# A hybrid attention/RG-LRU step on one core: gate halves evaluated in weight buffers, the first head group's values loaded beside its keys, background sums in 33 places in place of 36

## The chip, the cores and the metric

The kernel runs on one core of a Trainium2 chip. The metric is the device time of one execution in microseconds (us). A core has a matrix engine (TensorE, PE in the profile, with its weight loads as PEld), a vector engine (VectorE, DVE), a scalar engine (ScalarE, ACT), GpSimd (POOL) and SyncE (SP), which here issues most transfers. Each engine works through its own list of instructions in the order of the program and waits on semaphores that the others set.

## The reference

One inference step of two layers in float32. Layer 0 is grouped-query attention over 512 latent and 128 context tokens (16 heads, 4 key/value heads, width 2048), layer 1 a bidirectional gated linear recurrence. The part that the change touches is layer 0's projection, its gate, and the modulation vectors of layer 1, which need only the conditioning vector:

```
m = jax.nn.silu(cond) @ w_mod + b_mod
shift, scale, gate = jnp.split(m[:, None, :], 3, axis=-1)
...
p = h @ w_in
q, k, v, g = jnp.split(p, [ATTN_WIDTH, ATTN_WIDTH + KV_WIDTH, ATTN_WIDTH + 2 * KV_WIDTH], axis=-1)
q = rms_norm(q.reshape(b, n, N_HEADS, HEAD_DIM), q_norm)
k = rms_norm(k.reshape(b, n, N_KV_HEADS, HEAD_DIM), k_norm)
...
keys = jnp.concatenate([ck.astype(k.dtype), k], axis=1)
vals = jnp.concatenate([cv.astype(v.dtype), v], axis=1)
o = blocked_attention(q, keys, vals)
return (o * jax.nn.silu(g)) @ w_out
```

## The kernel before

**Arithmetic.** A float32 product is made of three matmuls: every operand is split into a rounded high part (`hi`, `wh`) and the rest (`lo`, `wl`), and `mm3` adds high x high (L184), and the two mixed products (L185, L186). The activations are split once and stay (`hi`, `lo`). A weight block of 1 MB is loaded by SP into one of four buffers `raw` (`load_w`), and `split_w` makes a high part on ACT (L179) and a low part on DVE (L180) of a half block (128 x 1024) into a ring of three pairs. PE reads these.

**Stages of layer 0's projection.** After the V projection come one K and four Q blocks (`gemm_nat`, four weight blocks each), then eight gate blocks (`gemm_T`, about 430 to 664 us), each of two weight blocks, that is four halves of 48 matmuls of 322 columns. A gate block has two accumulators of 128 gate channels, f = 0 and f = 1; in every half the 24 matmuls of f = 0 come first. Its evacuation `g_evac` computes (tanh(g/2) + 1) g for each f: ACT writes the tanh into a tile `qs` (L491), DVE multiplies into a tile `qf` (L492), and POOL issues the transfer of 322 KB into the scratch `g_s` (L493). `qs` and `qf` are two buffers each in the pool `pb`, shared with the norm and rotary work of K and Q. Then comes the attention: `attn_kv(j)` loads the keys of head group j into a `raw` buffer (`kx`) and its values into a tile of the pool `pc_` (`vx`), `attn_q` loads a head's queries and gate into a `raw` buffer; keys and queries are transposed on PE (L542, L571) and split, scores and softmax (L584 is the exponential) follow.

**Background.** `gemv` computes layer 1's shift and scale on DVE: 32 weight blocks of 1 MB from `w_mod`, in four sections of eight, four sums of 128 x 1024 to a block (L395). At a section's end the two accumulators are split and summed over the partitions by eight matmuls (L403), ACT copies a row (L406), PE transposes it (L408). `background()` is called after each of the 36 weight blocks of K, Q and the gates and takes 32/36 of a step each time; the rest of `gemv` is run after the last.

**What sets the order.** The program is written with pools and tiles; a scheduler lays the instructions of each engine in one list, the splits with higher priority, and inserts the semaphores. A buffer is given again when its last reader is done. So the order in each list depends on which tile waits for which.

Of the kernel before, what the change touches and what calls it, by code (L numbers as in the profile page):

```python
# [9 lines left out]
F32 = mybir.dt.float32  # L10
F32R = mybir.dt.float32r
BF16 = mybir.dt.bfloat16
AF = mybir.ActivationFunctionType
# [8 lines left out]
TW = 644  # L22
TH = TW // 2
# [21 lines left out]
def hybrid_step(ctx: ExitStack, tc: tile.TileContext, i, o):  # L45
    nc = tc.nc
    V, S, G, PE, SY = nc.vector, nc.scalar, nc.gpsimd, nc.tensor, nc.sync
    mult, add, sub = ALU.mult, ALU.add, ALU.subtract

    def pool(name, bufs, space=None, stack=None):  # L50
        kw = {} if space is None else {"space": space}
        return (stack or ctx).enter_context(
            tc.tile_pool(name=name, bufs=bufs, reuse_waits="tile", **kw))
# [3 lines left out]
    rawp = pool("rawp", 4)  # L57
# [6 lines left out]
    g_s = [tc.dram_tile([128, TW], F32, name=f"g_s{h}") for h in range(NH)]  # L64
# [6 lines left out]
    def ps1():  # L71
        return ps.tile([128, 512], F32, name="p1", tag="p1")
# [92 lines left out]
    scale = [cst.tile([128, KT, 2], F32, name=f"scale{l}") for l in range(2)]  # L165
# [68 lines left out]
    def gemm_T(w, col0, after=None):  # L234

        acc = [psd(), psd()]
        for kb in range(2):
            gemm_T_part(acc, load_w(w, kb * 1024, 8, col0, 256), kb * 8)
            if after:
                after()  # L240
        return acc
# [85 lines left out]
    with tc.manual_schedule():  # L327
# [5 lines left out]
        for n in range(9):  # L333
# [26 lines left out]
            if now:  # L360
                for f in range(2):
                    put(n * 2 + f, 0, xt[f], slice(0, NL))
                p = ps1()
# [13 lines left out]
    pb = pool("pb", 1, stack=xs)  # L377
# [45 lines left out]
    credit = [0.0]  # L423

    def background():
        credit[0] += 32 / 36
        while credit[0] >= 1:
            credit[0] -= 1
            next(gv, None)

    tab = {}
    for nm in ("rope_cos", "rope_sin"):
        t = pb.tile([128, 4, 128], F32, name=nm)
# [52 lines left out]

    def g_evac(acc, gb):
        for f in range(2):
            th = pb.tile([128, 2, 512], F32, name="qs", tag="qs", bufs=2)
            gg = pb.tile([128, 2, 512], F32, name="qf", tag="qf", bufs=2)  # L490
            S.activation(th[:, :, :TH], acc[f][:, :, :TH], AF.Tanh, scale=0.5)  # L491
            V.scalar_tensor_tensor(gg[:, :, :TH], th[:, :, :TH], 1.0, acc[f][:, :, :TH], op0=add, op1=mult)  # L492
            G.dma_start(g_s[gb * 2 + f].rearrange("p (h t) -> p h t", h=2), gg[:, :, :TH])  # L493

    for a, ms in zip(vacc, PAIRS):
        n = len(ms)
# [5 lines left out]
    pss.close()  # L502
    ps = pool("ps", 4, PSUM, stack=pss)
    norm_rope(gemm_nat(w_in, 2048, background), "k", k_s, o["new_cache_k"])
    for n in range(4):
        norm_rope(gemm_nat(w_in, n * 512, background), "q", q_s[:, n * 512:n * 512 + 512])
    for gb in range(8):
        g_evac(gemm_T(w_in, 3072 + gb * 256, background), gb)
# [9 lines left out]
    pc_ = pool("pc", 1, stack=xs)  # L518
# [6 lines left out]
    def psh():  # L525
        return psH.tile([128, 512], F32, name="ph", tag="ph")

    def attn_kv(j):
        c = slice(j * 128, j * 128 + 128)
        raw = rawp.tile([128, 2048], F32, name="raw", tag="raw")  # L530
        kx = raw[:, :896].rearrange("p (t d) -> p t d", d=128)
        vx = pc_.tile([128, 7, 128], F32, name="vx", tag="vx")
        for x, cache, scr in ((kx, "cache_k", k_s), (vx, "cache_v", v_s)):
            SY.dma_start(x[:, 0:2], i[cache][0, 0, :, j, :].rearrange("(t p) d -> p t d", p=128))
            SY.dma_start(x[:, 2:7], scr[:, c].rearrange("(t p) d -> p t d", p=128))
        kh = pc_.tile([128, 896], F32R, name="kh", tag="kh", bufs=2)
        kl = pc_.tile([128, 896], F32R, name="kl", tag="kl", bufs=2)
        for a, e in ((0, 4), (4, 7)):
            p = psh()
            n = (e - a) * 128  # L540
            for t in range(a, e):
                PE.transpose(p[:, (t - a) * 128:(t - a) * 128 + 128], kx[:, t], ident)  # L542
            d = slice(a * 128, e * 128)
            S.copy(kh[:, d], p[:, :n])
            V.tensor_tensor(kl[:, d], p[:, :n], kh[:, d].bitcast(F32), op=sub)
        return kh, kl, vx
# [130 lines left out]
    for h in range(NH):  # L677
        items += [(h, m) for m in range(4)]
        if h % 2:
            items.append((h, 4))  # L680
    done = {}
    kvs[0] = attn_kv(0)
    attn_q(0)
    attn_qt(0, 0, 4)
# [17 lines left out]
    def step_q(n):  # L702
        if n >= len(items):
            return
        h, m = items[n]
        nxt = h + 1
        if nxt < NH:
            if m == 3 and h % 4 == 3:
                kvs[nxt // 4] = attn_kv(nxt // 4)
            q0, q1, q2 = QO if h % 2 else QV  # L710
            if m == q0:
                attn_q(nxt)
            if m == q1:
                attn_qt(nxt, 0, 4)
            if m == q2:
                attn_qt(nxt, 4, 5)
# [164 lines left out]
    for blk in range(8):  # L881
# [21 lines left out]
        else:  # L903
            acc = gemm_T(w_l, blk * 256)
# [4 lines left out]
            acc = gemm_T(w_l, D + blk * 256)  # L909
# [6 lines left out]
        raw = rawp.tile([128, 2048], F32, name="raw", tag="raw")  # L916
# [5 lines left out]
        for f in range(2):  # L922
# [3 lines left out]
            for d in range(2):  # L926
                for g in range(2):
                    a = psd()
                    wh, wl = wg[g]
                    for k in range(2):  # L930
                        c0 = (d * 2 + k) * 256 + f * 128
                        for h in range(2):
                            t = slice(h * TH, h * TH + TH)
# [9 lines left out]
            for d in range(2):  # L943
# [12 lines left out]
                                 op0=mult, op1=add)  # L956
# [88 lines left out]
```

## Time and profile before

| | |
|---|---|
| runs (3) | 1956.23, 1958.24, 1959.07 us, median 1958.24 |
| the profiled execution | 1955.32 us |
| its span, from the first to the last instruction | 1953.6 us |
| mean granted clock of PE | 0.991 of full speed |
| PE busy | 1883.5 us, 96% |
| DVE busy | 1323.9 us, 68% |
| ACT busy | 865.0 us, 44% |

The profile is of one execution. Busy times leave out register, semaphore and transfer-issuing instructions. The bracket behind a row of the timeline is the idle time of that engine ahead of the instruction, with what ended it (`<-DVE wl L180`: the low part that DVE wrote at line 180). The line numbers are those of the kernel before. What ended a wait is inferred from semaphore events.

### The profile page before, as it was taken

To read this page: it belongs to the slowest core of one execution; us is meant where nothing else is said; L and a number is where in the kernel's file an instruction comes from. 1 tells how busy PE (TensorE), PEld (TensorE's weight loads), DVE (VectorE), ACT (ScalarE), POOL (GpSimd) and SP (SyncE) were. 2 spreads that over 40 slices of the span, in tenths; PEclk is the share of its full clock that TensorE was granted. 3 is DMA by queue.
4 is the path that set the end of the run, shared out by engine and by line. 5 is a ranking of instruction groups with operands and counts; after the bars stand their busy time and mean duration, and the time that the engine had idled before them with its cause. 6 is when DMAs were issued, how large, how long until landed. Compare 5 with 4: busy or idle time off the path is not lost.

```text
span 1953.6 us, 26764 instructions
## 1 busy us (share of the span) xinstructions
PE 1883.5 (96%) x10857; PEld 1673.2 (86%) x10857; DVE 1323.9 (68%) x1846; ACT 865.0 (44%) x1255; POOL 133.1 (7%) x212
## 2 busy tenths in 40 slices
PE   4999999999999899999999989899999999999996
PEld 1567887879999899998888889899999999987885
DVE  3237759758375389998857774875685675798645
ACT  4441223222121388881223565666456456742232
POOL 0000000000000001110000000110010010020000
PEclk9999999999999999999999999999999999999998
DMA  9996535536454212225636673323232232546445
GB/s 342 343 318 209 166 109 183 178 123 200 149 178 158 74 38 74 74 97 174 204 130 211 226 263 109 122 77 117 94 102 92 94 100 64 175 140 212 146 149 216
DMA packets 194892, 304.20 MB, mean 156 GB/s; under 512 B 7232, under 2 KB 124608, under 8 KB 191952
## 3 DMA queue, kind: packets, MB, share of 16 engines
q1 hardware_dynamic: 188800, 276.20, 42.6%
q0 software_dynamic: 5968, 26.28, 3.7%
q8 instruction: 85, 1.39, 0.3%
q14 instruction: 39, 0.32, 0.0%
HBM read 273.03 MB, written 29.43 MB: 155 GB/s over the span
## 4 chain that ended last, share of the span: by engine, by line
PE 83%; DVE 6%; ACT 5%; issue 2%; DMA 2%; SPq 1%; POOL 0%; DVEq 0%; ACTq 0%; POOLq 0%
PE pd L184 22%; PE pd L185 22%; PE pd L186 22%; PE pd L215 2%; PE pm L276 2%; PE pd L217 2%; PE pd L218 2%; PE ph L631 1%; PE pg L184 1%; ACT L937 1%; PE pg L186 1%; PE pg L185 1%; PE sp L184 1%; PE sp L186 1%; PE ph L184 1%
## 5 line engine op out<-in xcount | busy, mean ns | idle before, releaser
L179 ACT CAST wh<-raw 128x1024 fp32r<-128x1024 f32 x248 | 258.1, 1048 | 604.8 <-PE pd L186 323.6
L180 DVE TENSOR_TENSOR wl<-raw,wh 128x1024 fp32r<-128x1024 f32 x248 | 301.4, 1221 | 237.5 <-ACT wh L179 236.6
L184 PE MATMUL pd<-wh,hi 128*128 128x512 f32 x1040 | 410.4, 395 | 5.8 <-ACT pd L783 3.3
L185 PE MATMUL pd<-wl,hi 128*128 128x512 f32 x1040 | 409.9, 394 | 0.0
L186 PE MATMUL pd<-wh,lo 128*128 128x512 f32 x1040 | 409.7, 394 | 0.0
L184 PE MATMUL pd<-hi,wh 128*128 128x322 f32 x1280 | 399.2, 312 | 0.0
L186 PE MATMUL pd<-hi,wl 128*128 128x322 f32 x1280 | 397.0, 310 | 1.1 <-DVE wl L180 1.1
L185 PE MATMUL pd<-lo,wh 128*128 128x322 f32 x1280 | 397.5, 311 | 0.0
L186 PEld LDWEIGHTS pd<-hi,wl 128*128 128x128 f32 x1280 | 241.6, 189 | 1.6 <-DVE wl L180 1.6
L185 PEld LDWEIGHTS pd<-lo,wh 128*128 128x128 f32 x1280 | 242.2, 189 | 0.1
L184 PEld LDWEIGHTS pd<-hi,wh 128*128 128x128 f32 x1280 | 241.4, 189 | 0.5 <-ACT wh L179 0.3
L184 PEld LDWEIGHTS pd<-wh,hi 128*128 128x128 f32 x1040 | 195.5, 188 | 52.5 <-ACT pd L783 3.7
L186 PEld LDWEIGHTS pd<-wh,lo 128*128 128x128 f32 x1040 | 195.4, 188 | 45.9
L185 PEld LDWEIGHTS pd<-wl,hi 128*128 128x128 f32 x1040 | 195.4, 188 | 45.4 <-DVE wl L180 0.3
L741 DVE SCALAR_TENSOR_TENSOR ga<-raw,cT,ga 128x512 f32<-128x512 f32 x256 | 175.5, 744 | 15.2 <-DMA ga<-b_mod 12.4
L395 DVE SCALAR_TENSOR_TENSOR ga<-raw,cT,ga 128x1024 f32<-128x1024 f32 x120 | 149.7, 1278 | 28.1 <-DMA raw<-w_mod 27.5
L215 PE MATMUL pd<-hi,wh 128*128 128x256 f32 (+1 forms) x256 | 80.5, 314 | 6.4 <-ACT wh L179 4.7
L184 PE MATMUL pd<-xh,wh 128*128 128x322 f32 x256 | 81.1, 318 | 5.2 <-ACT xh L875 4.4
L185 PE MATMUL pd<-xl,wh 128*128 128x322 f32 x256 | 80.0, 313 | 0.0
L218 PE MATMUL pd<-hi,wl 128*128 128x256 f32 (+1 forms) x256 | 79.9, 312 | 0.0
L217 PE MATMUL pd<-lo,wh 128*128 128x256 f32 (+1 forms) x256 | 79.8, 312 | 0.0
L186 PE MATMUL pd<-xh,wl 128*128 128x322 f32 x256 | 79.8, 312 | 0.0
(233 smaller groups left out, 2807.3 us busy)
## 6 DMA issues: line engine op xcount, KB each, us to landing
raw<-w_mod SPq DMA_DIRECT2D x64, 1024.0 KB, 5.2
raw<-w_in_lru SPq DMA_DIRECT2D x40, 1024.0 KB, 5.3
raw<-w_in_attn SPq DMA_DIRECT2D x36, 1024.0 KB, 6.1
raw<-w_mod SPq DMA_DIRECT2D x64, 512.0 KB, 8.4
raw<-w_out_attn SPq DMA_DIRECT2D x20, 1024.0 KB, 6.0
raw<-w_out_lru SPq DMA_DIRECT2D x20, 1024.0 KB, 5.3
g_s<-qf POOLq DMA_DIRECT2D x16, 322.0 KB, 3.4
raw<-g_s SPq DMA_DIRECT2D x16, 322.0 KB
```

The source lines that it names most:

```text
L179: S.copy(wh, src)
L180: V.tensor_tensor(wl, src, wh.bitcast(F32), op=sub)
L184: PE.matmul(out, ah, bh, start=first, stop=False)
L185: PE.matmul(out, ah, bl, start=False, stop=False)
L186: PE.matmul(out, al, bh, start=False, stop=last)
L215: PE.matmul(outs[f], wh[:, c], hi[:, k, t], start=(k == 0 and first[f]), stop=False, skip_group_check=True)
L217: PE.matmul(outs[f], wh[:, c], lo[:, k, t], start=False, stop=False, skip_group_check=True)
L218: PE.matmul(outs[f], wl[:, c], hi[:, k, t], start=False, stop=(k == KT - 1), skip_group_check=True)
L276: PE.matmul(pm[32 * j:32 * j + 32], c32[:, kb * 4 + j], raw[:, j * 512:j * 512 + 512], start=(kb == 0), stop=(kb == 3))
L395: V.scalar_tensor_tensor(acc[c], w2[:, k2], cT[:, k, c:c + 1], acc[c], op0=mult, op1=add)
L631: PE.transpose(pt[:, c * 128:c * 128 + 128], P[:, b, c * 128:c * 128 + 128], ident)
L741: V.scalar_tensor_tensor(acc[:, c], raw[:, k4 * 512:k4 * 512 + 512], cT[:, kb * 4 + k4, c:c + 1], acc[:, c], op0=mult, op1=add)
```

## The change

Three edits. `background()` takes 32/33 of a step in place of 32/36, so that the sections of `gemv` end earlier: the last eight matmuls of each section (L403, L408) move from 301, 429, 561 and 664 us of the profiled execution to a place inside the second Q block, one inside the fourth, the boundary between the third and the fourth gate block, and the middle of the eighth. `g_evac` writes the tanh into a `raw` buffer and multiplies in place there; the transfer reads that buffer. And the values of head group 0 are loaded into the second half of the `raw` buffer that holds its keys.

```diff
--- before.py
+++ after.py
@@ -423,7 +423,7 @@
     credit = [0.0]
 
     def background():
-        credit[0] += 32 / 36
+        credit[0] += 32 / 33
         while credit[0] >= 1:
             credit[0] -= 1
             next(gv, None)
@@ -486,11 +486,10 @@
 
     def g_evac(acc, gb):
         for f in range(2):
-            th = pb.tile([128, 2, 512], F32, name="qs", tag="qs", bufs=2)
-            gg = pb.tile([128, 2, 512], F32, name="qf", tag="qf", bufs=2)
-            S.activation(th[:, :, :TH], acc[f][:, :, :TH], AF.Tanh, scale=0.5)
-            V.scalar_tensor_tensor(gg[:, :, :TH], th[:, :, :TH], 1.0, acc[f][:, :, :TH], op0=add, op1=mult)
-            G.dma_start(g_s[gb * 2 + f].rearrange("p (h t) -> p h t", h=2), gg[:, :, :TH])
+            gg = rawp.tile([128, 2048], F32, name="raw", tag="raw")[:, :TW].rearrange("p (h t) -> p h t", h=2)
+            S.activation(gg, acc[f][:, :, :TH], AF.Tanh, scale=0.5)
+            V.scalar_tensor_tensor(gg, gg, 1.0, acc[f][:, :, :TH], op0=add, op1=mult)
+            G.dma_start(g_s[gb * 2 + f].rearrange("p (h t) -> p h t", h=2), gg)
 
     for a, ms in zip(vacc, PAIRS):
         n = len(ms)
@@ -529,7 +528,10 @@
         c = slice(j * 128, j * 128 + 128)
         raw = rawp.tile([128, 2048], F32, name="raw", tag="raw")
         kx = raw[:, :896].rearrange("p (t d) -> p t d", d=128)
-        vx = pc_.tile([128, 7, 128], F32, name="vx", tag="vx")
+        if j == 0:
+            vx = raw[:, 896:1792].rearrange("p (t d) -> p t d", d=128)
+        else:
+            vx = pc_.tile([128, 7, 128], F32, name="vx", tag="vx")
         for x, cache, scr in ((kx, "cache_k", k_s), (vx, "cache_v", v_s)):
             SY.dma_start(x[:, 0:2], i[cache][0, 0, :, j, :].rearrange("(t p) d -> p t d", p=128))
             SY.dma_start(x[:, 2:7], scr[:, c].rearrange("(t p) d -> p t d", p=128))
```

Lines from `g_evac` on have moved: the tanh is L490 in place of L491, the product L491 in place of L492, and from `attn_kv` on a line number is higher by two.

Which instruction stands where in the engines' lists changes as follows. On ACT, around the boundary between the fifth and the sixth gate block, first of before. `qs` are the tanhs of the fifth block's f = 0 and f = 1; `raw_4294` and `raw_4406` are the sixth block's two weight blocks, so that the four `wh` are its four halves, and `raw_4530` belongs to the seventh.

```order
L179 CAST wh_4296<-raw_4294 128x1024
L406 COPY row_4149<-pd_4132 2x1024
L179 CAST wh_4348<-raw_4294 128x1024
L491 ACTIVATE qs_4282<-pd_4024 128x2x322
L179 CAST wh_4408<-raw_4406 128x1024
L491 ACTIVATE qs_4287<-pd_4025 128x2x322
L179 CAST wh_4460<-raw_4406 128x1024
L179 CAST wh_4532<-raw_4530 128x1024
```

The same place after the change, where the fifth block's tanhs write `raw_4292` and `raw_4296`, and the sixth block's weights are `raw_4302` and `raw_4414`:

```order
L179 CAST wh_4182<-raw_4180 128x1024
L179 CAST wh_4234<-raw_4180 128x1024
L490 ACTIVATE raw_4292<-pd_4066 128x644
L490 ACTIVATE raw_4296<-pd_4067 128x644
L179 CAST wh_4304<-raw_4302 128x1024
L179 CAST wh_4356<-raw_4302 128x1024
L179 CAST wh_4416<-raw_4414 128x1024
L179 CAST wh_4468<-raw_4414 128x1024
```

Before, three of the next block's four casts stand ahead of the second tanh; after, none does, and this holds at all seven boundaries between gate blocks.

On DVE at the same boundary, of before (`wl_4349` and `wl_4409` are the sixth block's second and third half; the sums L395 are the background's):

```order
L180 TENSOR_TENSOR wl_4349<-raw_4294,wh_4348 128x1024
L395 SCALAR_TENSOR_TENSOR ga1_4163<-raw_4512,cT_144,ga1_4163 128x1024
L395 SCALAR_TENSOR_TENSOR ga0_4162<-raw_4512,cT_144,ga0_4162 128x1024
L492 SCALAR_TENSOR_TENSOR qf_4283<-qs_4282,pd_4024 128x2x322
L395 SCALAR_TENSOR_TENSOR ga1_4163<-raw_4512,cT_144,ga1_4163 128x1024
L180 TENSOR_TENSOR wl_4409<-raw_4406,wh_4408 128x1024
L492 SCALAR_TENSOR_TENSOR qf_4288<-qs_4287,pd_4025 128x2x322
```

and after the change, where `wl_4305` is the sixth block's first half:

```order
L395 SCALAR_TENSOR_TENSOR ga1_3817<-raw_4286,cT_144,ga1_3817 128x1024
L491 SCALAR_TENSOR_TENSOR raw_4292<-raw_4292,pd_4066 128x644
L491 SCALAR_TENSOR_TENSOR raw_4296<-raw_4296,pd_4067 128x644
L180 TENSOR_TENSOR wl_4305<-raw_4302,wh_4304 128x1024
L180 TENSOR_TENSOR wl_4357<-raw_4302,wh_4356 128x1024
L395 SCALAR_TENSOR_TENSOR ga0_3816<-raw_4408,cT_144,ga0_3816 128x1024
L395 SCALAR_TENSOR_TENSOR ga1_3817<-raw_4408,cT_144,ga1_3817 128x1024
```

Both products now stand ahead of the first `wl` of the next block.

In SP's queue, from the last weight load to the attention's fourth head, of before (`raw_5074` takes the keys of head group 0, `vx_5075` its values, the `raw` with `q_s` and `g_s` the heads):

```order
L386 DMA raw_4994<-w_mod 128x2x1024
L534 DMA raw_5074<-cache_k 128x2x128
L535 DMA raw_5074<-k_s_95 128x5x128
L560 DMA raw_5095<-q_s_94 128x5x128
L562 DMA raw_5095<-g_s0_78 128x644
...
L562 DMA raw_5307<-g_s2_80 128x644
L560 DMA raw_5477<-q_s_94 128x5x128
L534 DMA vx_5075<-cache_v 128x2x128
L535 DMA vx_5075<-v_s_96 128x5x128
L562 DMA raw_5477<-g_s3_81 128x644
```

and after the change, where `vx_5721` takes the values of head group 1:

```order
L170 DMA raw_4900<-w_in_attn 128x8x256
L536 DMA vx_5721<-cache_v 128x2x128
L537 DMA vx_5721<-v_s_96 128x5x128
L536 DMA raw_5058<-cache_k 128x2x128
L537 DMA raw_5058<-k_s_95 128x5x128
L536 DMA raw_5058<-cache_v 128x2x128
L537 DMA raw_5058<-v_s_96 128x5x128
L562 DMA raw_5078<-q_s_94 128x5x128
L564 DMA raw_5078<-g_s0_78 128x644
```

The values of head group 0 moved from behind the fourth head's queries to directly behind the keys.

## Rows read from the trace of the kernel before

**Rows 1.** The head of the page: span, busy time of each engine (share of the span) and number of instructions; then the chain that ended last, by engine.
```profile
span 1953.6 us, 26764 instructions
...
PE 1883.5 (96%) x10857; PEld 1673.2 (86%) x10857; DVE 1323.9 (68%) x1846; ACT 865.0 (44%) x1255; POOL 133.1 (7%) x212
...
PE 83%; DVE 6%; ACT 5%; issue 2%; DMA 2%; SPq 1%; POOL 0%; DVEq 0%; ACTq 0%; POOLq 0%
```

**Rows 2.** Busy time by stretch, around the start of the first gate block and inside the gate blocks. Columns: stretch (us), its length, busy us (and instructions) of PE, its weight loads (PEld), DVE, ACT and POOL, granted clock of PE, share of the DMA engines, GB/s.
```profile
430.00:434.00 4.00, 2.91 (x22) 2.12 (x19) 4.00 (x5) 3.25 (x5) 0.00 (x0) 1.00 0.90 304
434.00:650.00 216.00, 216.00 (x1453) 214.42 (x1452) 128.30 (x141) 45.81 (x52) 11.61 (x17) 1.00 0.50 166
```

**Rows 3.** The timeline around the gate blocks: four rows of ACT, two of DVE, three of PE. Columns: start, us, engine, line, operation, output<-input and shapes; in brackets the idle time ahead of it and what ended that.
```profile
635.24 1.05 ACT L179 CAST wh<-raw 128x1024 fp32r<-128x1024 f32 x1 [2.69 <-PE pd L185]
636.19 0.70 ACT L491 ACTIVATE qs<-pd 128x644 f32<-128x644 f32 x1
642.34 1.05 ACT L179 CAST wh<-raw 128x1024 fp32r<-128x1024 f32 x1 [5.45 <-PE pd L185]
...
663.91 0.71 ACT L491 ACTIVATE qs<-pd 128x644 f32<-128x644 f32 x1 [2.84 <-PE pd L186]
...
643.42 1.23 DVE L180 TENSOR_TENSOR wl<-raw,wh 128x1024 fp32r<-128x1024 f32 x1 [5.14 <-ACT wh L179]
...
664.65 0.83 DVE L492 SCALAR_TENSOR_TENSOR qf<-qs,pd 128x644 f32<-128x644 f32 x1 [2.72 <-ACT qs L491]
...
432.39 0.42 PE L186 MATMUL pd<-hi,wl 128*128 128x322 f32 x1 [1.09 <-DVE wl L180]
432.64 0.32 PE L184 MATMUL pd<-hi,wh 128*128 128x322 f32 x1
...
663.57 0.31 PE L186 MATMUL pd<-hi,wl 128*128 128x322 f32 x1
```

**Rows 4.** The chain of waits, followed back from the last instruction, where the gate blocks end and the attention starts. Columns: start, us, what.
```profile
663.87 1.86 PE pd L403 x8
665.75 1.01 ACT row L406
...
668.40 0.36 SPq L560
668.80 0.53 SPq L534
669.38 4.97 DMA vx<-v_s
```

**Rows 5.** The timeline of the same stretch: three rows of PE, two of ACT, two of DVE (columns as in rows 3).
```profile
666.81 0.65 PE L408 MATMUL pd<-ident,row 2*128 2x2 f32 x8 [1.09 <-ACT row L406]
...
669.76 0.33 PE L571 MATMUL ph<-ident,raw 128*128 128x128 f32 x1 [0.85 <-DVE kl L545]
...
676.31 0.69 PE L184 MATMUL sp<-kh,wh 128*128 128x384 f32 x1 [3.79 <-ACT P L584]
...
674.43 0.94 ACT L552 CAST vh<-vx 128x896 fp32r<-128x896 f32 x1 [2.68 <-DMA vx<-v_s]
675.27 0.90 ACT L584 ACTIVATE P<-sp,mx 128x768 f32<-128x768 f32 x1
...
671.78 0.69 DVE L575 TENSOR_TENSOR wl<-ph,wh 128x512 fp32r<-128x512 f32 x1 [0.81 <-ACT wh L574]
672.39 1.81 DVE L581 TENSOR_REDUCE mx<-sp 128x1 f32<-128x768 f32 x2
```

**Rows 6.** Busy time by stretch behind longer waits of PE (columns as in rows 2; the granted clock is the third number from the end).
```profile
676.30:680.00 3.70, 3.69 (x12) 3.69 (x12) 2.65 (x4) 2.15 (x4) 1.24 (x1) 0.50 0.25 76
680.00:682.00 2.00, 2.00 (x12) 1.90 (x12) 1.41 (x3) 1.42 (x4) 0.00 (x0) 0.59 0.30 90
682.00:684.00 2.00, 2.00 (x16) 1.96 (x15) 1.49 (x3) 1.76 (x6) 0.00 (x0) 1.00 0.00 0
1224.30:1226.00 1.70, 1.68 (x9) 1.68 (x10) 1.67 (x2) 1.70 (x3) 0.10 (x1) 1.00 0.41 143
1768.70:1771.00 2.30, 2.24 (x10) 1.86 (x11) 1.01 (x2) 2.30 (x8) 0.31 (x1) 1.00 1.05 407
1137.30:1140.00 2.70, 2.63 (x13) 2.63 (x13) 2.65 (x4) 0.97 (x2) 0.00 (x0) 0.50 1.09 371
```

**Rows 7.** The timeline of PE: the first instruction behind the waits that rows 6 follow (the wait ahead of 676.31 stands in rows 5).
```profile
1224.32 0.44 PE L215 MATMUL pd<-hi,wh 128*128 128x388 f32 x1 [1.71 <-ACT I L937]
...
1768.76 0.50 PE L184 MATMUL pd<-wh,hi 128*128 128x512 f32 x1 [3.26 <-ACT pd L783]
...
1137.37 0.58 PE L215 MATMUL pd<-hi,wh 128*128 128x256 f32 x1 [4.73 <-ACT wh L179]
```

**Rows 8.** The timeline of POOL: the issue of a gate half's transfer.
```profile
662.22 0.69 POOL L493 DMA_DIRECT2D g_s<-qf  x1 [22.96 <-DVE qf L492]
```

**Rows 9.** DMA issues between 430 and 690 us. Columns: output<-input, queue, count, KB each, median us from issue to landing.
```profile
raw<-w_in_attn SPq DMA_DIRECT2D x14, 1024.0 KB, 6.5
...
g_s<-qf POOLq DMA_DIRECT2D x16, 322.0 KB, 3.4
...
raw<-q_s SPq DMA_DIRECT2D x4, 320.0 KB, 4.1
```

## The prediction

> **What bounds the kernel now.** The engine totals come first: TensorE (PE) is busy for 1883.5 of the 1953.6 us, DVE for 1323.9, ACT for 865.0, and the chain that ended last is PE for 83% [rows 1]. So the time moves where PE starts to wait or stops waiting. The busy time by stretch comes next, for the part that the change touches: from 434 to 650, inside the gate blocks, PE is busy for 216.00 of 216.00 us at full granted clock; in the 4 us ahead of that, where the first gate block starts, it is busy for 2.91 of 4.00 [rows 2]. The timeline of one gate split tells how PE is fed: ACT makes `wh` in 1.05, DVE starts `wl` 0.03 after that and takes 1.23, and ACT stood idle for 2.69 and 5.45 us before such casts, for a ring slot that PE still read (`<-PE pd L185`) [rows 3]. The splits run up to three halves ahead, and their time is hidden. The chain of waits shows where it is not full: from the end of the last gate block through the background sums, SP's late issue of the values, their 4.97 us of transfer and the first exponentials [rows 4].
>
> **Gate halves in weight buffers.** The arithmetic of an evacuation stays: a tanh of 0.71, a product of 0.83 [rows 3]. What moves is its place in two queues. In the order of before, ACT casts the next block's `wh` two or three halves ahead of a block's two tanhs. In the order after the change both tanhs stand ahead of the first cast of the next block, and on DVE both products ahead of its first `wl`, at the seven boundaries between gate blocks. The second tanh waits for the block's last matmul. So behind that wait are the next block's first cast, then its `wl`, and for `wl` PE.
>
> The stall from rows, with t0 the end of a block's last matmul (for the last block 663.57 + 0.31 = 663.88 [rows 3]): the tanh starts 0.03 later, lasts 0.71; an ACT instruction starts 0.10 before the one ahead of it ends (635.24 + 1.05 against 636.19 [rows 3]), so the cast runs from t0 + 0.64 to 1.69 and `wl` from 1.72 to 2.95; the matmul that needs `wl` follows about 0.04 after, at 2.99. Four matmuls that need only `wh` go before; unhindered, 0.15 apart (the next instruction starts 0.14 behind 663.57), the fifth would start at t0 + 0.42. That loses 2.57, and the first matmul after a wait takes 0.25 to the next one in place of 0.15 (432.39 and 432.64 [rows 3]): 2.65. Bounds: 2.3 if the four matmuls and ACT's overlap are worth more, 3.2 if each of three handovers costs 0.2 more. Six boundaries: 15.9. At the one from the third to the fourth gate block the background block L403/L408 now stands between: its row copy of 1.01 stands ahead of the cast on ACT, but PE has that block's own work meanwhile: 2.4. Together **+18.3**, from 16 to 22.
>
> Two other effects of the same edit I cost at nothing. The second weight load of a block now waits until the DMA of the preceding gate half has landed: issued 1.66 before t0 (662.22 [rows 8]), 3.4 to landing, then 6.5 for the load [rows 9], so the weights are there at t0 + 8.2; with 1.05 and 1.23 for the split they are ready at t0 + 10.5, and PE, with 96 matmuls at 0.15 to do first, wants them at t0 + 17. That cover of 6.5 us must go before anything is lost. On DVE the eight sums per block fit into the idle time as before.
>
> **Background in 33 places.** The four L403/L408 blocks are only moved: each occupies PE for 1.86 and 0.65, 2.5 together, anywhere [rows 4, 5]. One leaves the start of the first gate block: the wait of 1.09 for `wl` there [rows 3] and its restart go, **-1.1**. Two come into Q projections whose DVE is loaded with sums; no row shows them there, so 0 to 0.5 each by the one wait of this kind that is seen (1.09); I take **+0.5** for both, since each has a half ready ahead. One leaves the front of the attention for the middle of the last gate block, where it costs its own 2.5 again, and 0.1.
>
> **First values beside the keys, and the start of the attention.** SP issues the values only at 668.80 and 669.38, behind a Q load at 668.40 that waits for PE to have read the keys [rows 4]; ACT waits 2.68 for them in front of `vh` at 674.43, and the first exponential is held behind that until 675.27, PE until 676.31 [rows 5]. After the change they follow the keys in the queue, in the last gate block, tens of matmuls early. Gains, without the 2.5 that only moves:
> - the wait of 1.09 for the row copy [rows 5]: 1.1.
> - the first maximum ends about 673.3 (672.39 and half of 1.81), the exponential started at 675.27: 1.9.
> - that maximum stood behind the second head's `wl` at 671.78 [rows 5]; in the new order it stands ahead: 0.7, its 0.69.
> - PE idled for 3.79 and then had a granted clock of 0.50 for 3.7 us and 0.59 for 2.0 [rows 6]: 3.7 x 0.50 + 2.0 x 0.41 = 2.7 of PE time. The remaining wait, from the first twelve score matmuls to the first exponential's end, is about 1.3, and after 1.71 and 3.26 the clock stayed at 1.00 [rows 6, 7]: 2.6.
> - against that, `vh` (0.94) now runs between the keys' casts and the query's, where 0.85 was waited for `kl` anyway [rows 5]: -0.7.
>
> Together **-5.6**, from -4 to -7.5. The second head's Q load now waits for a gate half's DMA: 662.22 + 3.4 + 4.1 = 669.7 [rows 8, 9], with PE waiting for the exponential to about 670.4 anyway: nothing, at most 0.7.
>
> **Sum.** 18.3 - 1.1 + 0.5 + 0.1 - 5.6 = **+12.2**. The profiled execution took 1955.32, so 1967.5 by its own time; it lies 2.9 below the median of the runs, 1958.24, to which I add: **1970.4**. The likeliest case's own range is 16 - 1.1 - 7.5 = +7.4 to 22 + 1 - 4 = +19, 1965.6 to 1977.
>
> **Rivals.** First, the clock falls at the boundaries too. A boundary is two gaps, about 1.8 and 0.65, with four matmuls between them. For it: the clock was at 0.50 behind waits of 4.73 and 3.79 [rows 5 to 7]. Against it: 1.00 after 1.71 and 3.26 [rows 6, 7]; both gaps together are under 3.26, and PE was fully busy ahead of them. At 2.7 a time, seven give +19: 1989. [...]
>
> Second, the loads come late: if landing behind the gate halves takes over 6.5 us more, each further us costs six times; 1 us late gives +6, 1976, 2 give 1982. For it, 6.5 is a median and DMA is busy for 0.50 of the time there [rows 2]; against it, loads would have to take twice that in every block.
>
> Third, the other side, faster: the boundaries cost little because ACT's and DVE's queues have a half ready when a block ends, as the idle times of 2.69 and 5.45 show that they have time for. Then only the gains stay, -6.1: 1952. The new order speaks against it, since the cast stands behind a tanh that needs the last matmul. The seven boundaries break even with the gains at 0.9 each (6.1 / 7), less than the cast alone takes (1.05); faster by a measurable 3.9 it gets from 0.3 each down, and no change is what 0.3 to 1.4 each would give.
>
> **How the numbers follow.** The likeliest case 0.78, the clock 0.08, late loads 0.06, faster 0.05, no change 0.03. Taking 0.2% (3.9 us) as what a measurement here can tell from no change: slower 0.92, same 0.03, faster 0.05. The range runs from 1964, 2 below the likeliest case's low end for the scatter of the runs (1956.23 to 1959.07 before), to 1984, which takes in late loads and leaves out the clock and the cases without a loss.
>
> **What would show it.** Right: about 430 to 680, at six places 28 to 32 us apart, a PE wait for `wh` and one for `wl` (L186 `<-DVE wl L180`), about 2.4 us idle together, each with an ACT tanh just ahead; granted clock 1.00 there; gate blocks of about 31 us in place of 28.4, four halves of 7.1 (635.24 to 642.34 [rows 3]); PE's first score block within 3.5 us of the last gate matmul, no wait of 3.79, full clock in the ten us after. Wrong: boundaries without idle time (the third rival), a clock under 1.00 behind them (the first), a wait for `raw<-w_in_attn` in the middle of a block (the second), or a first exponential that still waits for `vh`.

## The result, and the profile after

The changed kernel takes 1973.61 us (median of four runs, 1969.75 to 1977.19) against 1958.6 before (1956.23 to 1959.07): ratio 1.0088, 95% interval 1.0074 to 1.0102. By these medians it is slower by 15 us, by the ratio by 17. Its four runs spread over 7.4 us and the four of before over 2.8, but 18 later runs of the kernel before lie between 1950.06 and 1961.25, so the spread says nothing by itself. The profiled execution took 1969.75, 14.4 more than that of before. PE's busy share stayed: 96%, as in [rows 1].

Three rows of the waits of PE over the whole execution, by what it waited for. Columns: engine, what waited, what for; us in total, times, the longest.

```profile
PE pd L184 <- ACT wh L179: 10.7, 7, 1.7
...
PE pd L186 <- DVE wl L180: 2.4, 6, 0.4
...
PE sp L184 <- ACT P L586: 2.3, 6, 0.9
```

The first two lines are new: seven waits for a cast and six for a low part, where before PE was busy without a break inside the gate blocks [rows 2]. The last one answers to the 3.79 ahead of 676.31 [rows 5]; its longest is now 0.9.

The timeline at the first boundary between gate blocks: PE, then ACT, then DVE.

```profile
459.20 0.30 PE L186 MATMUL pd<-hi,wl 128*128 128x322 f32 x1
461.24 0.41 PE L184 MATMUL pd<-hi,wh 128*128 128x322 f32 x1 [1.73 <-ACT wh L179]
461.49 0.31 PE L185 MATMUL pd<-lo,wh 128*128 128x322 f32 x1
461.63 0.31 PE L184 MATMUL pd<-hi,wh 128*128 128x322 f32 x1
461.78 0.31 PE L185 MATMUL pd<-lo,wh 128*128 128x322 f32 x1
462.50 0.42 PE L186 MATMUL pd<-hi,wl 128*128 128x322 f32 x1 [0.41 <-DVE wl L180]
...
459.54 0.71 ACT L490 ACTIVATE raw<-pd 128x644 f32<-128x644 f32 x1 [2.84 <-PE pd L186]
460.15 1.98 ACT L179 CAST wh<-raw 128x1024 fp32r<-128x1024 f32 x2
...
461.22 2.36 DVE L180 TENSOR_TENSOR wl<-raw,wh 128x1024 fp32r<-128x1024 f32 x2
```

One reads a chain from the left: the block's last matmul, 0.04 after its end the tanh, 0.10 before that one's end the cast, at its end the low part on DVE, and 0.05 after the first of these the matmul that needs it. The fifth matmul stands at 462.50; a pitch of 0.15 from 459.20 would have put it at 459.94. That is 2.56, and 0.25 to the next in place of 0.15: 2.66. Five other boundaries show the same two waits, 1.73 and 0.40 or 0.41.

The busy time by stretch, from one block's first matmul to the next block's, for the second and the fourth to sixth gate block, and behind two boundaries (columns as in [rows 2]).

```profile
461.20:492.40 31.20, 29.05 (x192) 28.53 (x192) 15.94 (x14) 5.42 (x7) 1.08 (x2) 1.00 0.48 157
...
525.70:529.30 3.60, 3.41 (x12) 3.00 (x13) 3.57 (x5) 0.96 (x2) 0.00 (x0) 0.54 0.67 213
525.70:558.00 32.30, 30.45 (x192) 29.78 (x192) 16.07 (x16) 5.40 (x8) 0.54 (x1) 0.95 0.41 142
...
560.00:563.60 3.60, 3.60 (x16) 3.60 (x15) 3.60 (x4) 0.70 (x1) 0.00 (x0) 0.53 0.84 293
558.00:590.70 32.70, 30.59 (x192) 30.07 (x192) 15.94 (x14) 5.38 (x8) 1.08 (x2) 0.95 0.44 149
590.70:621.90 31.20, 29.03 (x192) 28.51 (x192) 15.94 (x14) 5.43 (x8) 1.08 (x2) 1.00 0.47 157
```

A gate block with its boundary now takes 31.2, where four halves took 28.4 [rows 3]. The fourth and the fifth block take 1.1 and 1.5 more, and the two short stretches tell why: behind the third and the fourth boundary the granted clock is 0.54 and 0.53 for 3.6 us, that is nearly the lower of the two levels (1.2 of 2.4 GHz). PE's instructions are the same in number there, only longer, so the list of waits does not show this loss. PE's busy time does: 30.45 and 30.59 against 29.05, 1.4 and 1.5 more. (The length of the fourth block shows only 1.1 because that block starts without a wait for a low part.)

The attention's start: PE, then ACT.

```profile
685.23 0.92 PE L544 MATMUL ph<-ident,raw 128*128 128x128 f32 x7
...
688.36 0.44 PE L184 MATMUL sp<-kh,wh 128*128 128x384 f32 x1 [1.67 <-ACT wh L576]
...
692.15 0.44 PE L184 MATMUL sp<-kh,wh 128*128 128x384 f32 x1 [0.93 <-ACT P L586]
...
686.86 0.96 ACT L554 CAST vh<-raw 128x896 fp32r<-128x896 f32 x1
```

The keys' transposes follow the last gate matmul at once, `vh` runs without a wait, and the score matmul that stood at 676.31 behind 3.79 [rows 5] waits 0.93. The marks for the gain, two of before and one of after (the other is the first row above):

```profile
663.71 0.62 PE L403 MATMUL pd<-wh,sel 128*2 128x512 f32 x2
681.87 0.42 PE L184 MATMUL sp<-kh,wh 128*128 128x384 f32 x1
...
695.53 0.44 PE L184 MATMUL sp<-kh,wh 128*128 128x384 f32 x1 [0.26 <-ACT P L586]
```

From the first instruction behind the gates to the fifth block of score matmuls it took 18.2 before (663.71 to 681.87) and takes 10.3 now (685.23 to 695.53); less the 2.5 of the background block that only moved, 5.4 are gained.

### The profile page after: what moved, and what is told of

Same layout as the page of the kernel before. It is cut to its first block, busy times and chain, and to the rows that moved or that the text cites. A ratio compares the mean times of both kernels' runs of the same rounds, so it can differ in the third digit from the quotient of the medians.

```text
span 1968.0 us, 26754 instructions
## 1 busy us (share of the span) xinstructions
PE 1888.7 (96%) x10857; PEld 1674.3 (85%) x10857; DVE 1323.8 (67%) x1846; ACT 864.7 (44%) x1255; POOL 131.0 (7%) x212
## 4 chain that ended last, share of the span: by engine, by line
PE 83%; ACT 6%; DVE 6%; issue 2%; DMA 2%; SPq 1%; POOL 0%; DVEq 0%; ACTq 0%; POOLq 0%
PE pd L184 22%; PE pd L186 22%; PE pd L185 21%; PE pd L215 2%; PE pm L276 2%; PE pd L217 2%; PE pd L218 2%; PE ph L633 1%; PE pg L184 1%; DVE wl L180 1%; ACT L939 1%; PE pg L185 1%; PE pg L186 1%; PE ph L184 1%; PE ph L186 1%
## 5 line engine op out<-in xcount | busy, mean ns | idle before, releaser
L184 PE MATMUL pd<-hi,wh 128*128 128x322 f32 x1280 | 401.0, 313 | 10.7 <-ACT wh L179 10.7
L395 DVE SCALAR_TENSOR_TENSOR ga<-raw,cT,ga 128x1024 f32<-128x1024 f32 x120 | 148.7, 1280 | 19.2 <-DMA raw<-w_mod 18.9
```

The source lines that it names most:

```text
L184: PE.matmul(out, ah, bh, start=first, stop=False)
L395: V.scalar_tensor_tensor(acc[c], w2[:, k2], cT[:, k, c:c + 1], acc[c], op0=mult, op1=add)
```

## The experiments

Medians are compared with those of the kernel before, run beside them: 1955.19 for the kernels with edit 2 undone, edit 2 alone, the split first and the tanh twice, 1956.58 for the four others.

**Edit 2 undone.** The changed kernel with `g_evac` as before:

```diff
-            gg = rawp.tile([128, 2048], F32, name="raw", tag="raw")[:, :TW].rearrange("p (h t) -> p h t", h=2)
-            S.activation(gg, acc[f][:, :, :TH], AF.Tanh, scale=0.5)
...
+            th = pb.tile([128, 2, 512], F32, name="qs", tag="qs", bufs=2)
+            gg = pb.tile([128, 2, 512], F32, name="qf", tag="qf", bufs=2)
+            S.activation(th[:, :, :TH], acc[f][:, :, :TH], AF.Tanh, scale=0.5)
...
```

(`...` stands for lines left out: here the product and the transfer.)

> Edits 1 and 3 without edit 2: background in 33 places and the first values beside the keys, gate halves evaluated in qs and qf as before. Theory (the cast of the next block stands behind the block's last tanh in the changed kernel, and that alone makes it slower): three casts stand ahead of the second tanh again, no PE wait at the gate boundaries; what is left is the first gate block's wait (-1.1) and the attention's start (-5.3 in the changed kernel's trace), some +0.3 for the moved sums: 6 us faster than before, about 1952.5. Rival (the loss comes from the moved background sums or from the transfers that edit 3 puts in the queue): a loss of some 10 us or more stays, 1968 or above.

Measured: 1949.83, ratio 0.9972 (0.9961 to 0.9983), 5.4 us faster than before. The gate blocks in its busy time by stretch:

```profile
433.00:650.00 217.00, 217.00 (x1457) 214.75 (x1456) 114.95 (x128) 47.30 (x55) 11.61 (x17) 1.00 0.44 146
650.00:666.00 16.00, 16.00 (x109) 15.10 (x107) 3.54 (x5) 2.75 (x4) 0.69 (x1) 1.00 0.24 75
```

PE does not wait once from the first gate block to the last, and the clock is 1.00. So the other two edits together are a gain of about the forecast size (6.1 by the prediction's terms), and the whole loss hangs on edit 2.

**Edit 2 alone,** in the kernel of before:

```diff
-            th = pb.tile([128, 2, 512], F32, name="qs", tag="qs", bufs=2)
-            gg = pb.tile([128, 2, 512], F32, name="qf", tag="qf", bufs=2)
+            gg = rawp.tile([128, 2048], F32, name="raw", tag="raw")[:, :TW].rearrange("p (h t) -> p h t", h=2)
...
```

> Edit 2 alone: gate halves in weight buffers, everything else as before. Theory (queue order): seven boundaries at 2.66 without a background block among them, +18.6, and 1.5 more for each boundary behind which the granted clock is low (two of seven in the changed kernel's profiled execution): +18.6 to +29, 1977 to 1988. Rival (the loss is not edit 2's): within 3 us of before, 1956 to 1961. Rival (edit 2 also makes loads late, which the other edits cover): above 1988, with waits for raw<-w_in_attn in the middle of a block.

Measured: 1987.36, ratio 1.0168 (1.0152 to 1.0184), +32, which is 3 more than the upper end of the loss expected. Three rows of its waits of PE:

```profile
PE pd L184 <- ACT wh L179: 12.2, 7, 1.8
PE pd L186 <- DVE wl L180: 7.1, 9, 3.2
PE pd L403 <- ACT wh L179: 6.3, 1, 6.3
```

The boundaries are there, seven at 1.7 to 1.8 and 0.41, and the clock is low behind three of them, the third, fifth and seventh. But two waits are new. One is 3.19 in the middle of the fifth block, for a low part that stands in DVE's list behind sums that waited 5.61 for `raw<-w_mod`. SP had held that load back for 5.3 us, for the transfer of a gate half out of the same buffers. The other is 6.32 ahead of the last L403, whose sums stand behind the last two gate products in DVE's order. Behind both the granted clock is at the lower level:

```profile
578.10:584.90 6.80, 6.75 (x28) 6.40 (x29) 1.49 (x4) 0.00 (x0) 0.00 (x0) 0.50 0.85 307
698.70:707.80 9.10, 7.71 (x29) 4.20 (x29) 3.94 (x7) 3.49 (x5) 0.00 (x0) 0.50 0.64 198
```

So a load does come late behind a gate half once, with 36 places for the sums. It is a load of the sums, though, not the `raw<-w_in_attn` by which the prediction's second rival was to be known. With 33 places, as in the full change, PE has no such wait. Inside the gate blocks the terms add up: boundaries 18.6, three low stretches behind them some 4.5, the 3.19, and some 3 for the low clock behind it make 29.3, and the trace loses 29.2 there. Some 5 more come at the start of the attention: the 6.32 and the low clock behind it cost more there than the waits of before that they replace, 1.09, 0.85 and 3.79 [rows 5].

**The split ahead of the evacuation.** All three edits, with the next block's first half split first (`gemm_T_part` takes the pair that is ready as `pre`):

```diff
...
-    for gb in range(8):
-        g_evac(gemm_T(w_in, 3072 + gb * 256, background), gb)
+    pre, raw0 = None, load_w(w_in, 0, 8, 3072, 256)
+    for gb in range(8):
+        acc = [psd(), psd()]
+        gemm_T_part(acc, raw0, 0, pre)
+        background()
+        gemm_T_part(acc, load_w(w_in, 1024, 8, 3072 + gb * 256, 256), 8)
+        background()
+        if gb < 7:
+            raw0 = load_w(w_in, 0, 8, 3072 + (gb + 1) * 256, 256)
+            pre = split_w(raw0[:, :1024])
+        g_evac(acc, gb)
```

> All three edits, gate halves in weight buffers, but the program splits the first half of the next gate block's weights ahead of the evacuation, so that its first two casts stand ahead of both tanhs in ACT's list. Theory (queue order): no boundary waits, the gains of edits 1 and 3 stay: about 6 us faster than before, 1952.5, granted clock 1.00 in the gate blocks. Rival (the buffers, not the order: four raw buffers do not do for weights, sums and gate halves together): waits of PE stay at the boundaries or go to the middle of the blocks, with DMA as what ended them; 1966 or above.

Measured: 1951.91, ratio 0.9981 (0.997 to 0.9993), 3.3 faster than before. Its busy time by stretch:

```profile
434.00:650.00 216.00, 216.00 (x1452) 214.38 (x1452) 116.91 (x125) 46.40 (x53) 9.58 (x17) 1.00 0.46 151
```

The gate halves still lie in weight buffers, and their transfers still hold those buffers. PE does not wait. ACT's timeline at the first boundary:

```profile
454.75 1.06 ACT L179 CAST wh<-raw 128x1024 fp32r<-128x1024 f32 x1 [4.01 <-PE pd L185]
...
458.42 0.71 ACT L490 ACTIVATE raw<-pd 128x644 f32<-128x644 f32 x1 [1.31 <-PE pd L186]
461.97 0.71 ACT L490 ACTIVATE raw<-pd 128x644 f32<-128x644 f32 x1 [2.85 <-PE pd L186]
462.58 1.04 ACT L179 CAST wh<-raw 128x1024 fp32r<-128x1024 f32 x1
```

One cast stands ahead of the two tanhs, not two as the expectation has it, and one is enough. The edit also asks for the next block's first weight buffer ahead of the two for the gate halves. But that load was not what the changed kernel waited for: there the cast starts 0.10 before the tanh ends. So it is not that gate halves lie in weight buffers that costs the time, but the place of two tanhs ahead of a cast. It stays about 2 us behind the kernel with edit 2 undone; its trace loses 1.7 in the first heads of the attention, as the changed kernel's does.

**A longer wait at the boundary.** The changed kernel with the second tanh of each block computed twice, and then three times, into the same buffer (`range(2 ...)` for three times):

```diff
             S.activation(gg, acc[f][:, :, :TH], AF.Tanh, scale=0.5)
+            for _ in range(1 if f else 0):
+                S.activation(gg, acc[f][:, :, :TH], AF.Tanh, scale=0.5)
```

> The changed kernel with the second tanh of each gate block computed twice into the same buffer, 0.62 us more on ACT between a block's last matmul and the next cast. Theory (queue order): each of six boundaries waits 0.62 longer, the seventh and the attention's start up to that: +3.7 to +5 against the changed kernel if the clock behaves as there. Second question, the clock behind such waits: if its fall depends on the length of the wait, the low clock shows behind more boundaries than the changed kernel's two, 1.5 us each: up to +7.5 more, 1986 in all; if it does not, it stays at two or so and the time is near 1978. Rival (the cast is held by something else, a load or a ring slot): no change against 1973.6.

> The changed kernel with the second tanh of each gate block computed three times into the same buffer: the wait ahead of the next cast grows from 2.47 (twice) to about 3.2. Theory (the low clock comes with the length of the wait): behind all seven boundaries and perhaps the attention's start, against six of seven at 2.47 and two or three of seven at 1.73; against the run with the tanh twice +0.74 at seven boundaries and +1.5 at one, some +6. Rival (the low clock is a matter of chance that does not depend on the wait): two to six boundaries, +5 from the waits alone, more or less 3.

**The changed kernel once more,** as a second profile:

> The changed kernel once more, unchanged, as the measure for the runs beside it and as a second profile. Its first four runs lay between 1969.75 and 1977.19 with granted clocks of 0.991 to 0.988. If the low clock behind a boundary is a matter of chance at a wait of 1.73 and 0.41, the profile shows it behind other boundaries than the third and the fourth, and the runs spread again by some 1.5 us per such boundary: 1965 to 1978, median near 1971. If it hangs on the work at those two places, the same two show it, and the runs lie within 3 us of each other.

Measured: 1985.59 with the tanh twice, 1990.63 with it three times, and 1974.19 (1971.48 to 1975.42; ratio 1.0091, 1.0077 to 1.0105) for the kernel as it is. The ratios of the other two are 1.0153 (1.0139 to 1.0167) and 1.0177 (1.0163 to 1.0191). The waits of PE for the cast, first as it is, then twice, then three times:

```profile
PE pd L184 <- ACT wh L179: 10.7, 7, 1.7
```

```profile
PE pd L184 <- ACT wh L179: 15.1, 7, 2.5
```

```profile
PE pd L184 <- ACT wh L179: 19.5, 7, 3.2
```

Where the granted clock is low behind a boundary is seen in busy time by stretch. Of the second profile of the changed kernel, three of seven, the first, third and fourth:

```profile
463.00:466.20 3.20, 3.20 (x12) 3.20 (x13) 3.20 (x3) 0.00 (x0) 0.00 (x0) 0.52 1.03 343
494.20:500.00 5.80, 5.33 (x34) 5.07 (x35) 5.76 (x5) 2.01 (x3) 0.54 (x1) 1.00 0.72 238
527.60:531.00 3.40, 3.40 (x12) 3.06 (x13) 3.40 (x4) 0.87 (x1) 0.00 (x0) 0.51 0.48 145
...
561.00:565.00 4.00, 4.00 (x17) 4.00 (x18) 4.00 (x4) 0.00 (x0) 0.00 (x0) 0.58 0.94 316
592.40:598.00 5.60, 5.14 (x33) 4.88 (x34) 5.57 (x5) 1.40 (x2) 0.54 (x1) 1.00 0.81 249
```

The rows at 494 and 592, at 1.00, are the second and the fifth boundary, which are not hit. The first boundary is hit here and was not in the first profile; the third and the fourth are hit in both. The four runs lie within 3.9 us, so they do not decide between the two expectations. With the tanh twice, at 2.47, it is six of seven; the fifth boundary, at 601 us, is the exception. With it three times, at 3.21, all seven; here four of them:

```profile
463.50:467.00 3.50, 3.47 (x13) 3.25 (x14) 3.49 (x4) 1.28 (x2) 0.54 (x1) 0.56 0.95 340
497.00:501.00 4.00, 3.94 (x15) 3.53 (x16) 4.00 (x4) 1.71 (x2) 0.54 (x1) 0.57 0.78 284
...
599.00:603.20 4.20, 3.83 (x15) 3.53 (x16) 4.20 (x4) 1.96 (x2) 0.54 (x1) 0.59 0.76 276
...
666.90:671.40 4.50, 4.06 (x16) 3.80 (x17) 3.50 (x3) 1.89 (x2) 0.54 (x1) 0.62 0.30 106
```

The third boundary stands apart, with the background block between waits of 1.09 to 1.32 and 0.3: it is hit in all four profiles of these kernels. Of the plain ones, 1.73 long, one of six and two of six are hit in the two profiles of the changed kernel and three of seven with edit 2 alone, 6 of 19 together; of those 2.47 long five of six, of those 3.21 long six of six.

The same is seen at two other places, which no edit aimed at. At the start of the K block, at 150 us, PE waits 1.50 to 2.09 in seven of the ten profiles, and the clock stays at 1.00; in three it waits 2.50, 2.71 and 3.29, and the clock falls. At the place of the 3.26 of [rows 7], at 1763 to 1801 us, it waits between 2.74 and 3.84: with 3.17 or more the clock falls in five of six profiles, the kernel before being the sixth, and below that in one of four. This one is the run with the tanh twice:

```profile
1798.21 0.67 PE L184 MATMUL pd<-wh,hi 128*128 128x512 f32 x1 [2.74 <-ACT pd L787]
```

```profile
1798.40:1801.80 3.40, 3.40 (x9) 2.66 (x9) 1.27 (x2) 2.65 (x8) 1.30 (x2) 0.50 1.05 401
```

The wait of 1.71 of [rows 7], with no other close to it, is 1.68 to 1.71 in all ten profiles and is hit in none. So something besides the length, the 0.41 behind the 1.73 or the work around the two, has a part in the boundaries' falls; no run here separates it.

So each boundary does wait for the cast behind the tanh (0.74 for each tanh more), and the low clock comes more often the longer the wait. The first step adds 5.0 of waits at the boundaries (15.1 - 10.7, and 0.6 for `wl`), 0.7 at the attention's start, and three or four low stretches of 1.5: some 11, measured 11.4 against the kernel as it is (1974.19); 1986 was expected if the fall depends on the length. For the second step +6 was expected, and it was +5.0. By the ratios to the kernel before, which was run beside each, the two steps are 12 and 5.

**Edit 1 alone and edit 3 alone,** each in the kernel of before:

```diff
-        credit[0] += 32 / 36
+        credit[0] += 32 / 33
```

> Edit 1 alone, background in 33 places: gate halves and first values as before. From before's rows: the first gate block's wait of 1.09 goes (-1.2 with the restart), the wait of 1.09 for the row copy at the attention's start goes (-1.1), the moved sums cost up to 0.5; the first exponential still waits for the values, and whether the wait stays long enough for the low clock behind it is open: -1.5 to -2.5, or, if what is gained is only waited away for the values, -0.7. If edit 3 matters little, all of the 5 to 6 us that edits 1 and 3 gain together come here.

```diff
-        vx = pc_.tile([128, 7, 128], F32, name="vx", tag="vx")
+        if j == 0:
+            vx = raw[:, 896:1792].rearrange("p (t d) -> p t d", d=128)
+        else:
+            vx = pc_.tile([128, 7, 128], F32, name="vx", tag="vx")
```

> Edit 3 alone, the first values beside the keys: background in 36 places, gate halves as before. From before's rows: the first exponential 1.9 earlier, 0.7 for the maximum, 2.6 for the clock, less 0.7 for the cast of the values between those of keys and queries: -4.5. If the attention's start is held by the background block in front of it, nothing: within 1 of before.

Measured: edit 1 alone 1955.91, ratio 0.9998 (0.9989 to 1.0006), no difference clear of noise (0.7 faster by the medians, the smaller of the two gains that were expected); edit 3 alone 1953.2, ratio 0.9989 (0.9979 to 0.9998), 2 to 3 us faster, where 4.5 was expected. With both it is 5.4. The two parts alone make 3 to 4; that is less than 5.4, but within what these intervals leave open, so it is the traces that tell more. Of edit 1 alone, ACT's timeline in front of the first exponential, and the busy time by stretch behind it:

```profile
675.12 0.94 ACT L552 CAST vh<-vx 128x896 fp32r<-128x896 f32 x1 [3.89 <-DMA vx<-v_s]
```

```profile
677.00:680.00 3.00, 3.00 (x9) 3.00 (x10) 2.35 (x4) 1.77 (x3) 1.23 (x1) 0.50 0.17 49
```

The background block is gone from the front, and the wait for the values has grown from 2.68 [rows 5] to 3.89: what edit 1 gives there is waited away. (Its other gain is in the trace: at the first gate block the wait of 1.09 [rows 3] is gone.) Of edit 3 alone, the same stretch:

```profile
673.50:676.00 2.50, 2.46 (x8) 2.46 (x9) 1.22 (x4) 1.85 (x3) 0.00 (x0) 0.55 0.74 249
676.00:679.00 3.00, 3.00 (x20) 2.97 (x19) 2.15 (x4) 1.98 (x4) 0.00 (x0) 0.81 0.00 1
```

The values are there, PE waits only 1.87 for the exponential, and yet the clock is low behind it: waits of 1.09 for the row copy and 0.53 for a key's low part stand shortly ahead. In the four profiles that have both edits and each tanh once, it is 1.00 there. Since such falls come at some executions and not at others, one profile of edit 3 alone does not show that the clock is always low there.

## Why the prediction came out right, and where its sizes were off

The forecast was 1970.4, the measurement 1973.6, within the range. (The upper end of the likeliest case, +19, leaves out the -1.1 of the first gate block; with it, it is +18.) By the two profiled executions, forecast +12.2 against 14.4:

- **The boundaries.** Forecast 2.65 each, measured 2.66 at six. At the one from the third to the fourth block, with L403/L408 in it, PE waited 1.09 and 0.30 and lost about 1.5 where 2.4 were put. The chain of tanh, cast and low part was the right mechanism, and the split put ahead of the evacuation shows that its place in the queue is the cause.
- **The first gate block.** Forecast -1.1 + 0.5. Third matmul of the block: 432.39 before, 431.12 after; with 0.6 for L408, which before has yet to come there, and 0.6 by which the after trace is early at 146 us already, -1.3. The moved sums made no wait in the Q blocks.
- **The clock at the boundaries.** This is the term that was missing: 1.4 and 1.5 at two boundaries, +2.9. The first rival was put as all seven or none, 2.7 each, at a chance of 0.08. What occurs is some of seven, another number in each profile, 1.5 each; that is about as much as the median lies above the forecast. The mean granted clock goes with it: the fastest of the first four runs shows 0.991, the slowest 0.988. The step that failed is the one that took 1.71 and 3.26 without a fall [rows 6, 7] as proof that shorter waits leave the clock alone. One profile can't bear that: at the very place of the 3.26 the clock fell in six of the ten profiles, while at that of the 1.71 it held in all. The Trainium skill's page "TensorE: Matmul & The Clock Gate", section "HAM oscillation", describes bursts of matmuls that each start at the slow clock, behind waits for data of about 3 to 5 us. The traces agree in kind (0.51 to 0.62 behind the waits that are hit), and show such falls behind 1.7 to 3.2 us too, in a share of places that grows with the wait.
- **The attention's start.** Forecast -5.6, measured -5.4. Its parts were not additive in the traces, though: edit 1's 1.1 there is waited away without edit 3, and in the one profile of edit 3 without edit 1 the clock was low behind the first exponential, so that the clock term of 2.6 was not there in full.
- **Not foreseen.** In the first heads of the attention the trace after loses another 1.65 (13.67 behind before at the first product of probabilities and values, 15.32 at the last), about 1.0 of it in three PE waits of 0.3 to 0.4 for `ptl` and `kl`. The kernel with the split first loses it too, the one with edit 2 undone does not. It was not traced further; that it comes from the other order of loads and splits there is argued, not shown.
- **The sum.** That it came as close as 2.2 is partly luck: the clock (+2.9) and the loss not foreseen (+1.65) are about half made up for by the boundary with L403/L408 (-0.9), by the first gate block (-0.7) and by the 0.6 by which the after trace was early before any of it.
- **The rivals.** Late loads did not hold PE up in the full change; with edit 2 alone one load of the sums did. The faster one was excluded by the boundaries' 2.66, against the 0.9 from which gains and losses break even.

## What to carry to other kernels

Where an evacuation shares a rotating set of buffers with the operands of the next block, look up in each engine's list whether the next block's preparation still stands ahead of it: here the same instructions in another order cost 2.66 us per block, and emitting the next block's first split before the evacuation took those waits away. A new short wait of PE in a dense stretch should be priced with the chance of a slow stretch behind it, as one cost more, and two edits at one point of waiting are to be summed by what waits next, not each by its own row. The faster version that came out is the change without its second edit, 0.9972 of before.

## What the runs showed that was not expected

A wait of 1.73 us and one of 0.41 right behind it bring the granted clock down to about half for some 3.5 us in 6 of 19 places, some 1.5 us each, and not always at the same ones; at 2.47 it is five of six, at 3.21 all. The kernel before has such places too: the 3.26 of [rows 7] was not hit in its own profile, and waits of 2.74 to 3.84 at that place were hit in six of the ten. At the attention's start 1.87 behind 1.09 and 0.53 brought the clock down, and so did 3.15; 1.29 and 1.38, 1.67 and even 2.41 did not.
